# A table of C with one power of lambda more, and one product in place of two in a state-space scan

## The chip, the cores and the metric

The kernel runs on one core of a Trainium2 chip. Its time is the device time of one execution in microseconds (us). The engines of a core run their own instruction streams side by side and wait for each other by semaphores: TensorE (PE, matrix products), VectorE (DVE), ScalarE (ACT), GpSimd (POOL), and SyncE (SP), which here only issues transfers. POOL and ACT can issue transfers too. Each stream, and each queue of transfers issued from it, goes in order.

## The reference

Two layers of a streaming encoder. Each layer is half a feed-forward block, a mixer, and half a feed-forward block. In layer 0 the mixer is a diagonal state space (S5) beside attention. The change is in the S5 part:

```python
lam_bar = jnp.exp(lam * jnp.exp(log_step.astype(f32))[:, None])
b_bar = ((lam_bar - 1.0) / lam)[..., None] * lax.complex(b_re.astype(f32), b_im.astype(f32))
bu = jnp.einsum('gpc,btgc->btgp', b_bar, uf.astype(b_bar.dtype))
...
_, hs = lax.associative_scan(_lin_rec, (jnp.broadcast_to(lam_bar, bu.shape), bu), axis=1)
c = lax.complex(c_re.astype(f32), c_im.astype(f32))
y = jnp.einsum('gcp,btgp->btgc', c, hs).real + d.astype(f32).reshape(G_A, S5_GROUP) * uf
```

There are 32 groups of 16 channels with 64 complex states each.

## The kernel before, in words

The scan over time runs on blocks of four tokens. A state is carried from block to block, and what happens inside a block is put into tables that depend on the weights alone: E (powers of lambda times B-bar, 3 down to 0), C (C times the powers 1 to 4 of lambda), D (the response inside a block, C times powers 0 to 3 of lambda times B-bar, laid out as a block triangle), and cosines and sines for the rotation of the states. Sixteen pairs of groups have a table each. `s5_tables` (line 951) makes one and stores it in device memory (`S`); `s5_scan` (line 1017) later reads two at a time.

The tables are made beside the first feed-forward block (`ffn(0, 0, beside=...)` in `build`), whose inner loop runs 19 times through `head` (line 617, about 14.5 us each). After each head one step of the generator `tables()` is taken; `s5_tables` yields once, so that the second half of table e and the first half of table e+1 are recorded behind the same head. After four heads (three in the last groups) comes the output product `wout` (line 664), 35 us long. The order of the instructions within the engines' streams is set by a scheduler of the framework from its own estimates, not by the text alone; the listing below shows it.

The steps of a table, by line:

- 963, 964: two loads, on SP's queue, of B and C of this pair into `bc`.
- 969 (`cmul`, lines 875 to 880): six operations on POOL make B-bar (`bb`, 32 columns), with `tb` for scratch.
- 974: six operations on POOL make `E` (128 columns, scratch `tE`).
- 977: POOL makes `nci`, minus the imaginary part of C. 979: six operations on POOL write C into the table's tile `tab`.
- 986 to 992: ACT (L990) and DVE make the angles; 999: ACT writes cosine and sine into `tab`, 1000: POOL copies a part of them.
- 1005: two transposes of E on PE, 1006: ACT copies them into `tab`.
- 1010 to 1012: PE multiplies `bb` by C: power 0, straight from `bc` and `nci`, as 32 columns, and powers 1 to 3, from `tab`, as 96. Each has a real and an imaginary part: four matmuls in fp32, of two pieces each.
- 1014: four copies on ACT spread the result over the block triangle of D.
- 1015: POOL issues the store of `tab`.

`tab`, `bc`, `bb`, `nci` and the scratch tiles have one buffer each (`bufs=1`), so a table's step waits until the table before is done with the tile.

The lines of `head` that the text speaks of: ACT's copy at L637 hands a partial result on and frees PE's bank for the product of `S3` (L648, recorded as L550); DVE's L660 and L661 and ACT's L662 finish the head before. L460, L461 and L464 are the products of `unit_k` in `wout`, L321 and L322 the split of weights by ACT and DVE, and L373 the load of weights on SP's queue.

Of the kernel before, what the change touches and what calls it, by code (L numbers as in the profile page):

```python
# [26 lines left out]
NS = 173  # L27
# [11 lines left out]
def _layout(*items):  # L39
    d, o = {}, 0  # L40
    for n, k in items:
        d[n] = (o, k)
        o += k
    d["_n"] = o
    return d
# [8 lines left out]
C0 = _layout(("ident", 128), ("diag16", 16))  # L54
CA = _layout(("slot", 133), ("live", NS), ("msel", 1))
CB = _layout(("dbase", 528), ("dsamp", 528), ("dmeta", 16), ("cmb", 128))
CD = _layout(("tri", 128), ("tri16", 16), ("edge", 64), ("cos", 96), ("sin", 96), ("samp", 8))
SCAN = _layout(("ET", 256), ("C0", 128), ("C1", 128), ("D", 128), ("cos", NS), ("sin", NS))


def shape_constants():
# [209 lines left out]
class Kern:  # L271
# [679 lines left out]
    def s5_tables(self, pool, e):  # L951

        nc = self.nc
        v, g = nc.vector, nc.gpsimd
        P2 = slice(e, e + 1)

        def tl(name, sh, bufs=1, dt=F):
            return pool.tile([128] + sh, dt, name="st_" + name, tag=name, bufs=bufs)

        tab = tl("tab", [SCAN["_n"]])  # L960
        sub = lambda n: tab[:, SCAN[n][0]:SCAN[n][0] + SCAN[n][1]]
        bc = tl("bc", [4, 1, 32])
        nc.sync.dma_start(bc[:, 0:2], self.io["s5b"][:, :, P2])
        nc.sync.dma_start(bc[:, 2:4], self.io["s5c"][:, :, P2])

        bb = tl("bb", [2, 1, 32])
        tb = tl("tb", [1, 32])
        bx = lambda a: a[:, P2, None].to_broadcast([128, 1, 32])
        self.cmul(g, (bb[:, 0], bb[:, 1]), (bc[:, 0], bc[:, 1]), (bx(self.s5_co[0]), bx(self.s5_co[1])), tb)
        E = [tl(f"E{i}", [1, 4, 32]) for i in range(2)]  # L970
        tE = tl("tE", [1, 4, 32])
        ex = lambda a: a[:, P2, :, None].to_broadcast([128, 1, 4, 32])
        bxx = lambda a: a[:, :, None, :].to_broadcast([128, 1, 4, 32])
        self.cmul(g, E, (bxx(bb[:, 0]), bxx(bb[:, 1])), (ex(self.s5_rv[0]), ex(self.s5_rv[1])), tE)

        nci = tl("nci", [1, 32])
        g.tensor_scalar(nci, bc[:, 3], -1.0, None, op0=OP.mult)
        C = [sub(f"C{i}").rearrange("p (a j c) -> p a j c", a=1, j=4) for i in range(2)]
        self.cmul(g, C, (bxx(bc[:, 2]), bxx(nci)), (ex(self.s5_pw[0][:, :, 1:5]), ex(self.s5_npi[:, :, 1:5])), tE)
        D = sub("D").rearrange("p (a j c) -> p a j c", a=1, j=4)  # L980
        g.memset(D, 0.0)

        f0, f1, f2 = [tl(f"f{i}", [133]) for i in range(3)]
        th = slice(e, e + 1)

        def wrap(x):
            v.tensor_scalar(f1, x, MAGIC, MAGIC, op0=OP.add, op1=OP.subtract)
            v.tensor_tensor(x, x, f1, op=OP.subtract)

        nc.scalar.activation(f0, self.ca["slot"], AF.Copy, scale=self.s5_th[:, th])  # L990
        wrap(f0)
        v.scalar_tensor_tensor(f0, self.ca["slot"], self.s5_tl[:, th], f0, op0=OP.mult, op1=OP.add)
        v.tensor_scalar(f2, f0, 0.25, None, op0=OP.add)
        wrap(f0)
        wrap(f2)
        yield
        for n, x in (("cos", f2), ("sin", f0)):
            c = sub(n)
            nc.scalar.activation(c[:, 0:133], x, AF.Sin, scale=2.0 * PI_LIM)
            g.tensor_copy(c[:, 133:].rearrange("p (s k) -> p s k", k=5), c[:, None, 0:5].to_broadcast([128, 8, 5]))  # L1000

        pt = self.btile()[:, :256].rearrange("p (i a k) -> p i a k", i=2, a=1)
        for i in range(2):
            for a in range(1):
                nc.tensor.transpose(pt[:, i, a], E[i][:, a].rearrange("p i c -> p (i c)"), self.ident)
        nc.scalar.copy(sub("ET"), pt.rearrange("p i a k -> p (i a k)"))

        pk = self.btile()
        pkv = pk[:, :128].rearrange("p (a j c) -> p a j c", a=1, j=4)
        for j, c in ((0, (bc[:, 2, 0], nci[:, 0])), (1, [sub(f"C{i}")[:, 0:96] for i in range(2)])):  # L1010
            for i in range(2):
                nc.tensor.matmul(pk[:32, 32 * j:32 if j == 0 else 128], bb[:, i, 0], c[i], start=i == 0, stop=i == 1)
        for i in range(4):
            nc.scalar.copy(D[32 * i:32 * i + 32, :, i:4], pkv[:32, :, 0:4 - i])
        nc.gpsimd.dma_start(self.dram["S"][e], tab)

    def s5_scan(self, pool, e, U, G):

        nc = self.nc
        v, g = nc.vector, nc.gpsimd  # L1020
        P2 = slice(2 * e, 2 * e + 2)
        c4, pp0 = e // 2, 2 * (e % 2)

        def tl(name, sh, bufs=1, dt=F):
            return pool.tile([128] + sh, dt, name="sc_" + name, tag=name, bufs=bufs)

        tab = tl("tab", [2, SCAN["_n"]], 2)
        nc.sync.dma_start(tab, self.dram["S"][P2].rearrange("a p n -> p a n"))
        sub = lambda n: tab[:, :, SCAN[n][0]:SCAN[n][0] + SCAN[n][1]]
        ET = sub("ET").rearrange("p a (i k) -> p i a k", i=2)  # L1030
        C = [sub(f"C{i}") for i in range(2)]
        D = sub("D")
        cs = [sub(n) for n in ("cos", "sin")]
        u4 = tl("u4", [2, NS], 2)
        for i in range(4):
            nc.sync.dma_start(u4[32 * i:32 * i + 32],
                              U[c4, pp0 * 32:pp0 * 32 + 64, i].rearrange("(a c) s -> c a s", a=2))

        Z = [tl(f"Z{i}", [2, NS], 2) for i in range(2)]
        for i in range(2):  # L1040
            b = self.btile()
            for a in range(2):
                nc.tensor.matmul(b[:, a * NS:a * NS + NS], ET[:, i, a], u4[:, a], start=True, stop=True)
            nc.scalar.copy(Z[i].rearrange("p a s -> p (a s)"), b[:, :2 * NS])
        yield

        W = [tl(f"W{i}", [2, NS], 2) for i in range(2)]
        tmp = tl("tmp", [2, NS])
        sh = lambda t: t[:, :, 0:NS - 1]
        up = lambda t: t[:, :, 1:NS]  # L1050
        self.cmul(v, (up(W[0]), up(W[1])), (sh(Z[0]), sh(Z[1])), (up(cs[0]), up(cs[1])), sh(tmp), conj_b=True)
        for i, nm in enumerate(("h0re", "h0im")):
            g.memset(W[i][:, :, 0:1], 0.0)
            h0 = self.p[nm].rearrange("p (a b) -> p a b", b=8)
            g.tensor_copy(W[i][:, :, 133::5], h0[:, P2])
        mul = tl("mul", [2, NS])
        for a in range(2):
            v.tensor_scalar(mul[:, a], self.ca["live"], self.s5_r4[:, 2 * e + a:2 * e + a + 1], None, op0=OP.mult)
        fl = lambda t: t.rearrange("p a s -> p (a s)")
        for i in range(2):  # L1060
            v.tensor_tensor_scan(fl(W[i]), fl(mul), fl(W[i]), 0.0, op0=OP.mult, op1=OP.add)
        self.cmul(v, Z, W, cs, tmp)
        yield
        for i in range(2):
            g.tensor_copy(self.s5o[:, i, P2, 0:1], Z[i][:, :, 132:133])
            g.tensor_copy(self.s5o[:, i, P2, 1:9], Z[i][:, :, 137::5])
        b = self.btile()
        for a in range(2):
            q = b[:, a * NS:a * NS + NS]
            for i in range(2):  # L1070
                nc.tensor.matmul(q, C[i][:, a], Z[i][:, a], start=i == 0, stop=False)
            nc.tensor.matmul(q, D[:, a], u4[:, a], start=False, stop=True)
        y = tl("y", [2, NS], 2)
        for a in range(2):
            v.scalar_tensor_tensor(y[:, a], u4[:, a], self.p["d"][:, 2 * e + a:2 * e + a + 1], b[:, a * NS:a * NS + NS],
                                   op0=OP.mult, op1=OP.add)
        nc.scalar.activation(y, y, AF.Gelu_apprx_tanh)
        for j in range(4):
            nc.sync.dma_start(G[c4, pp0 * 32:pp0 * 32 + 64, j].rearrange("(a c) s -> c a s", a=2),
                              y[32 * j:32 * j + 32])  # L1080
        yield
# [923 lines left out]
def build(tc, io, stage=99, dbg=None):  # L2005
# [17 lines left out]
              "G": dr.tile([4, 128, 4, NS], F, name="G"), "LF": dr.tile([T, 8], F, name="LF"),  # L2023
              "M": dr.tile([128, 4, T], F, name="M"), "S": dr.tile([16, 128, SCAN["_n"]], F, name="S"), "FC": dr.tile([72, 528], F, name="FC"),
              "Q": dr.tile([8, 96, T], F, name="Q"), "K": dr.tile([8, 96, NP], F, name="K"),
# [354 lines left out]
```

## Time and profile before

| what | value |
|---|---|
| median of 3 runs | 2690.78 us (2679.24 to 2692.4) |
| the profiled execution | 2691.17 us |
| its span | 2689.0 us |
| PE busy | 2601.6 us, 97% of the span |
| DVE busy | 1958.2 us, 73% |
| ACT busy | 1169.4 us, 43% |
| POOL busy | 258.6 us, 10% |
| mean granted clock of PE | 0.989 of full speed |
| PE busy between 60 and 490 us | 417.67 of 430 us |

The span is what the profiler saw of the engines; the time of the execution is 2.17 us more. Almost all of the span is PE's own work, so its gaps are what other engines can cost. The chain of work that ended last is 81% PE, 7% DVE, 4% transfers, 2% POOL and 2% ACT. The tables' part on POOL lies in the first 470 us.

### The profile page before, as it was taken

Reading aid. Unit: us, or ns where it says so; the run is one execution under the profiler, and the core shown is the slowest. Engines: PE = TensorE matmul, PEld = TensorE weight load, DVE = VectorE, ACT = ScalarE, POOL = GpSimd, SP = SyncE. Lnnn points to the kernel's source line nnn. Section 1 sums busy time; section 2 is a strip of 40 time slices with the busy share of each in tenths; the row PEclk is TensorE's granted clock in tenths of the full one; section 3 lists DMA queues with packets and bytes.
Section 4 is the critical chain, followed back from the end, with each engine's and each line's share of the span. In section 5 each row is a group of like instructions: output and inputs, shape, how many; then the busy total and the mean of one; then the engine's idle time right before and its main releaser. Section 6 shows DMA issues by size and latency. Waiting matters only on the chain.

```text
span 2689.0 us, 45288 instructions
## 1 busy us (share of the span) xinstructions
PE 2601.6 (97%) x17467; PEld 2437.3 (91%) x17467; DVE 1958.2 (73%) x4011; ACT 1169.4 (43%) x2125; POOL 258.6 (10%) x572
## 2 busy tenths in 40 slices
PE   8999999998899999999999999999988999999999
PEld 8999999877679999999999999987766779999999
DVE  8778777887686867776887677766666667686776
ACT  6344444334553534333543334344544654343333
POOL 1046434031000000000000000002000100000000
PEclk9999999999999999999999999999998899999999
DMA  4233322545753222222222222244565532222222
GB/s 140 75 105 94 100 92 89 193 144 163 253 181 108 84 75 84 77 79 79 83 75 83 79 79 78 87 135 106 153 197 183 163 107 79 87 81 84 85 81 79
DMA packets 133172, 295.86 MB, mean 110 GB/s; under 512 B 30244, under 2 KB 55156, under 8 KB 128668
## 3 DMA queue, kind: packets, MB, share of 16 engines
q1 hardware_dynamic: 129516, 280.72, 33.6%
q0 software_dynamic: 2720, 10.78, 1.2%
q8 instruction: 138, 2.26, 0.3%
q10 hardware_dynamic: 720, 1.45, 0.2%
q14 instruction: 78, 0.64, 0.1%
HBM read 257.05 MB, written 34.21 MB: 108 GB/s over the span
## 4 chain that ended last, share of the span: by engine, by line
PE 81%; DVE 7%; DMA 4%; issue 4%; POOL 2%; ACT 2%; SPq 0%; DVEq 0%; ACTq 0%; POOLq 0%
PE pa L550 7%; PE pa L551 6%; PE pa L552 6%; PE pd L460 4%; PE pw L460 4%; PE pw L464 4%; PE pd L461 4%; PE pd L464 4%; PE pw L461 4%; PE pc L551 3%; PE pc L550 3%; PE pc L552 3%; PE pmm L464 2%; PE pmm L330 2%; PE pmm L461 2%
## 5 line engine op out<-in xcount | busy, mean ns | idle before, releaser
L321 ACT CAST whi<-wraw 128x1024 fp32r<-128x1024 f32 (+3 forms) x426 | 336.2, 790 | 654.8 <-PE pw L461 213.3
L322 DVE TENSOR_TENSOR wlo<-wraw,whi 128x1024 fp32r<-128x1024 f32 (+3 forms) x426 | 385.5, 906 | 132.8 <-ACT whi L321 126.4
L460 PE MATMUL pd<-gh,whi 128*128 128x328 f32 (+1 forms) x704 | 215.4, 313 | 0.5 <-ACT gh L321 0.3
L461 PE MATMUL pw<-gl,whi 128*128 128x328 f32 (+1 forms) x704 | 214.7, 312 | 0.0
L461 PE MATMUL pd<-gl,whi 128*128 128x328 f32 (+1 forms) x704 | 214.3, 312 | 0.0
L460 PE MATMUL pw<-gh,whi 128*128 128x328 f32 (+1 forms) x704 | 214.2, 311 | 0.0
L464 PE MATMUL pd<-gh,wlo 128*128 128x328 f32 (+1 forms) x704 | 162.8, 311 | 0.0
L464 PE MATMUL pw<-gh,wlo 128*128 128x328 f32 (+1 forms) x704 | 161.9, 311 | 0.0
L321 ACT CAST wvh<-wu 128x1024 fp32r<-128x1024 f32 x79 | 83.0, 1050 | 153.0 <-PE pc L551 150.7
L460 PEld LDWEIGHTS pd<-gh,whi 128*128 128x128 f32 x704 | 131.8, 188 | 3.4 <-ACT gh L321 1.4
L460 PEld LDWEIGHTS pw<-gh,whi 128*128 128x128 f32 x704 | 132.2, 188 | 0.2 <-issue 0.2
L461 PEld LDWEIGHTS pw<-gl,whi 128*128 128x128 f32 x704 | 132.3, 188 | 0.0
L461 PEld LDWEIGHTS pd<-gl,whi 128*128 128x128 f32 x704 | 132.0, 188 | 0.3 <-DVE gl L322 0.3
L672 DVE SCALAR_TENSOR_TENSOR mo<-pd,mo 128x328 f32<-128x328 f32 (+1 forms) x120 | 54.0, 492 | 106.3 <-PE pd L464 105.7
L330 PE MATMUL pmm<-whi,hh 128*128 128x512 f32 (+2 forms) x328 | 126.6, 389 | 2.3 <-ACT whi L321 2.3
L331 PE MATMUL pmm<-wlo,hh 128*128 128x512 f32 (+2 forms) x328 | 124.6, 380 | 0.8 <-DVE wlo L322 0.6
L332 PE MATMUL pmm<-whi,hl 128*128 128x512 f32 (+2 forms) x328 | 123.5, 376 | 0.0
L672 DVE SCALAR_TENSOR_TENSOR mo<-pw,mo 128x328 f32<-128x328 f32 (+1 forms) x120 | 54.0, 492 | 95.2 <-PE pw L464 95.1
L464 PEld LDWEIGHTS pd<-gh,wlo 128*128 128x128 f32 x704 | 118.9, 188 | 0.2 <-DVE wlo L322 0.2
L464 PEld LDWEIGHTS pw<-gh,wlo 128*128 128x128 f32 x704 | 118.8, 188 | 0.0
L550 PE MATMUL pa<-ht,wzh 128*128 128x328 f32 (+1 forms) x316 | 99.6, 315 | 6.1 <-ACT u L637 6.1
L550 PE MATMUL pa<-hh,whi 128*128 128x328 f32 (+1 forms) x316 | 100.6, 318 | 0.0
(659 smaller groups left out, 8042.5 us busy)
## 6 DMA issues: line engine op xcount, KB each, us to landing
wraw<-wi SPq DMA_DIRECT2D x97, 512.0 KB
wu<-wi SPq DMA_DIRECT2D x79, 512.0 KB
wraw<-wo SPq DMA_DIRECT2D x104, 256.0 KB
wraw<-wo SPq DMA_DIRECT2D x48, 320.0 KB
row<-dkT SPq DMA_DIRECT2D x8, 1024.0 KB
wraw<-ckT SPq DMA_DIRECT2D x16, 512.0 KB
row<-dv SPq DMA_DIRECT2D x8, 1024.0 KB
row<-fkT SPq DMA_DIRECT2D x8, 1024.0 KB
```

The lines of the kernel that those rows point to most:

```text
L321: nc.scalar.copy(hi, src)
L322: nc.vector.tensor_tensor(lo, src, hi.bitcast(F), op=OP.subtract)
L330: mm(ps, a[0], b[0], start=start, stop=False)
L331: mm(ps, a[0], b[1], start=False, stop=False)
L332: mm(ps, a[1], b[0], start=False, stop=stop)
L460: mm(ps[b], hi[:, ws], xh[:, c], start=start, stop=False)
L461: mm(ps[b], hi[:, ws], xl[:, c], start=False, stop=False)
L464: mm(ps[b], lo[:, ws], xh[:, c], start=False, stop=stop)
L550: nc.tensor.matmul(p[:, A], w[0][:, c], xh, start=start and i == 0, stop=False, skip_group_check=True)
L551: nc.tensor.matmul(p[:, A], w[0][:, c], xl, start=False, stop=False, skip_group_check=True)
L552: nc.tensor.matmul(p[:, A], w[1][:, c], xh, start=False, stop=i == 3, skip_group_check=True)
L672: v.scalar_tensor_tensor(self.x[:, o, c], p[b][:, A], 0.5, self.x[:, o, c], op0=OP.mult, op1=OP.add)
```

## The change

C gets power 0 of lambda too: five powers of 32 columns, 160 in place of 128, for the real and for the imaginary part. So the six operations at line 979 work on 160 columns, and `tE` is 160 wide. PE's product of `bb` and C then takes the first 128 of these columns (powers 0 to 3) in one piece for each part: two matmuls of 128 columns in place of two of 32 and two of 96, and none reads `bc` or `nci`. The table grows from 986 to 1050 numbers for each partition. `s5_scan` takes columns 32 to 160 of C (powers 1 to 4, as before).

```diff
-SCAN = _layout(("ET", 256), ("C0", 128), ("C1", 128), ("D", 128), ("cos", NS), ("sin", NS))
+SCAN = _layout(("ET", 256), ("C0", 160), ("C1", 160), ("D", 128), ("cos", NS), ("sin", NS))
...
-        C = [sub(f"C{i}").rearrange("p (a j c) -> p a j c", a=1, j=4) for i in range(2)]
-        self.cmul(g, C, (bxx(bc[:, 2]), bxx(nci)), (ex(self.s5_pw[0][:, :, 1:5]), ex(self.s5_npi[:, :, 1:5])), tE)
+        C = [sub(f"C{i}").rearrange("p (a j c) -> p a j c", a=1, j=5) for i in range(2)]
+        ex, bxx = [lambda a, f=f: f(a, 5) for f in (ex, bxx)]
+        self.cmul(g, C, (bxx(bc[:, 2]), bxx(nci)), (ex(self.s5_pw[0]), ex(self.s5_npi)), tE)
...
-        for j, c in ((0, (bc[:, 2, 0], nci[:, 0])), (1, [sub(f"C{i}")[:, 0:96] for i in range(2)])):
-            for i in range(2):
-                nc.tensor.matmul(pk[:32, 32 * j:32 if j == 0 else 128], bb[:, i, 0], c[i], start=i == 0, stop=i == 1)
+        for i in range(2):
+            nc.tensor.matmul(pk[:32, :128], bb[:, i, 0], sub(f"C{i}")[:, 0:128], start=i == 0, stop=i == 1)
...
-        C = [sub(f"C{i}") for i in range(2)]
+        C = [sub(f"C{i}")[:, :, 32:160] for i in range(2)]
```

(After the change the lines from 980 to the transposes stand one number higher; the product keeps its number, 1012.)

The order on POOL, from the end of C of table 1 to the first half of E of table 2, before:

```order
L880 TENSOR_TENSOR st_tab<-st_tab,st_tE 128x128
L1000 COPY st_tab<-st_tab 128x40 x2
L1015 DMA S<-st_tab 128x986
L875 TENSOR_TENSOR st_bb<-st_bc,s_cor 128x32
L876 TENSOR_TENSOR st_tb<-st_bc,s_coi 128x32
L878 TENSOR_TENSOR st_bb<-st_bc,s_cor 128x32
L877 TENSOR_TENSOR st_bb<-st_bb,st_tb 128x32
L977 TENSOR_SCALAR st_nci<-st_bc 128x32
L879 TENSOR_TENSOR st_tb<-st_bc,s_coi 128x32
L875 TENSOR_TENSOR st_E_1810<-st_bb,s_rv_945 128x128
L880 TENSOR_TENSOR st_bb<-st_bb,st_tb 128x32
L876 TENSOR_TENSOR st_tE<-st_bb,s_rv_946 128x128
```

and the same place after the change:

```order
L880 TENSOR_TENSOR st_tab<-st_tab,st_tE 128x160
L1001 COPY st_tab<-st_tab 128x40 x2
L876 TENSOR_TENSOR st_tb<-st_bc,s_coi 128x32
L977 TENSOR_SCALAR st_nci<-st_bc 128x32
L875 TENSOR_TENSOR st_bb<-st_bc,s_cor 128x32
L878 TENSOR_TENSOR st_bb<-st_bc,s_cor 128x32
L877 TENSOR_TENSOR st_bb<-st_bb,st_tb 128x32
L879 TENSOR_TENSOR st_tb<-st_bc,s_coi 128x32
L875 TENSOR_TENSOR st_E_1806<-st_bb,s_rv_945 128x128
L880 TENSOR_TENSOR st_bb<-st_bb,st_tb 128x32
L876 TENSOR_TENSOR st_tE<-st_bb,s_rv_946 128x128
L1015 DMA S<-st_tab 128x1050
```

The store of table 1 has moved behind nine operations of table 2.

The order on SP around the first loads of an output product, with the semaphores that each waits for (PE, Pool and DVE by their engine, DMAHW for a transfer), before:

```order
L373 DMA wraw<-wo 128x512 [waits DMAHW6_49,DVE_49]
L963 DMA st_bc<-s5b 128x2x32 [waits DMAHW4_49,DMAHW5_49,PE_49,Pool_49]
L964 DMA st_bc<-s5c 128x2x32 [waits DMAHW3_49]
L373 DMA wraw<-wo 128x512 [waits DMAHW7_49,DVE_49]
L373 DMA wraw<-wo 128x512 [waits DMAHW1_49,DVE_49]
```

and the same place after:

```order
L373 DMA wraw<-wo 128x512 [waits DMAHW6_49,DVE_49]
L963 DMA st_bc<-s5b 128x2x32 [waits DMAHW1_49,DMAHW0_49,Pool_49]
L373 DMA wraw<-wo 128x512 [waits DMAHW7_49,DMAHW5_49,DVE_49]
L964 DMA st_bc<-s5c 128x2x32
L373 DMA wraw<-wo 128x512 [waits DMAHW3_49,DVE_49]
```

The load of `bc` waits for POOL and no longer for PE, and its second half has moved behind a load of weights.

## Rows read from the trace of the kernel before

**Rows 1.** The page, section 1: busy us, share of the span, instructions.

```profile
PE 2601.6 (97%) x17467; PEld 2437.3 (91%) x17467; DVE 1958.2 (73%) x4011; ACT 1169.4 (43%) x2125; POOL 258.6 (10%) x572
```

**Rows 2.** Waits of PE, 130 to 470 us: total us, times, longest us.

```profile
PE pa L550 <- ACT u L637: 6.1, 7, 1.6
PE pb L1012 <- POOL st_tab L880: 3.5, 2, 2.2
```

**Rows 3.** The chain of waits, 205 to 262 us: start us, us, what.

```profile
208.84 0.22 PE pb L1005 x2
209.06 0.57 PE pb L1012 x8
...
211.12 5.58 DMA S<-st_tab
216.81 0.53 ACT st_tab L999 x2
217.36 0.42 ACT st_f L990
217.80 0.42 DVE st_f L987
...
221.13 0.75 ACT gs L662
221.88 0.33 ACT u L637
222.25 0.42 PE pa L550
```

**Rows 4.** Waits of ACT, 130 to 470 us.

```profile
ACT whi L321 <- PE pd L461: 34.4, 15, 3.0
...
ACT st_tab L999 <- DMA S<-st_tab: 9.3, 9, 2.0
```

**Rows 5.** Waits of DVE, 130 to 470 us.

```profile
DVE st_f L987 <- ACT st_f L990: 8.4, 10, 1.6
```

**Rows 6.** The store's line, L1015: what its engine waited for, and the landing.

```profile
  ACT st_tab L1014: 211.9, 15
...
DMA to landing us min/median/max: 3.1/3.6/5.6
```

**Rows 7.** Groups of instructions, POOL, 130 to 470 us: busy us, mean ns | idle before.

```profile
L876 POOL TENSOR_TENSOR st_tE<-st_bb,s_rv 128x128 f32<-128x128 f32 x15 | 8.6, 574 | 1.1
...
L875 POOL TENSOR_TENSOR st_E<-st_bb,s_rv 128x128 f32<-128x128 f32 x15 | 6.8, 456 | 0.0
...
L878 POOL TENSOR_TENSOR st_bb<-st_bc,s_cor 128x32 f32<-128x32 f32 x15 | 5.2, 350 | 0.0
...
L877 POOL TENSOR_TENSOR st_bb<-st_bb,st_tb 128x32 f32<-128x32 f32 x15 | 5.2, 345 | 0.0
L880 POOL TENSOR_TENSOR st_bb<-st_bb,st_tb 128x32 f32<-128x32 f32 x15 | 4.9, 328 | 0.0
L879 POOL TENSOR_TENSOR st_tb<-st_bc,s_coi 128x32 f32<-128x32 f32 x15 | 4.4, 292 | 0.1
L875 POOL TENSOR_TENSOR st_bb<-st_bc,s_cor 128x32 f32<-128x32 f32 x15 | 4.4, 292 | 5.9 <-DMA st_bc<-s5b 5.6
```

**Rows 8.** Timeline of POOL, a busy and a quiet stretch: start us, us, what.

```profile
227.25 0.29 POOL L875 TENSOR_TENSOR st_bb<-st_bc,s_cor 128x32 f32<-128x32 f32 x1
...
232.95 0.45 POOL L878 TENSOR_TENSOR st_E<-st_bb,s_rv 128x128 f32<-128x128 f32 x1
...
243.60 0.25 POOL L875 TENSOR_TENSOR st_bb<-st_bc,s_cor 128x32 f32<-128x32 f32 x1
...
245.91 0.40 POOL L878 TENSOR_TENSOR st_E<-st_bb,s_rv 128x128 f32<-128x128 f32 x1
```

**Rows 9.** Three windows: stretch, its us, busy us of each engine, PEclk, DMA share, GB/s.

```profile
222.00:226.00 4.00, 3.75 (x28) 3.42 (x29) 3.97 (x8) 3.58 (x9) 1.34 (x2) 1.00 0.42 131
241.00:245.00 4.00, 3.90 (x16) 3.73 (x17) 1.76 (x5) 0.86 (x5) 2.36 (x11) 0.57 0.58 177
245.00:249.00 4.00, 4.00 (x28) 4.00 (x27) 1.51 (x3) 2.21 (x6) 3.69 (x10) 1.00 0.08 32
```

**Rows 10.** Waits of SP's queue, 130 to 470 us.

```profile
SPq L963 <- PE pb L1012: 30.8, 11, 8.0
```

More of the change, by code (lines that the diff above doesn't have):

```diff
@@ L970, in s5_tables @@
         E = [tl(f"E{i}", [1, 4, 32]) for i in range(2)]
[L971 to L974, printed above, removed]
+        tE = tl("tE", [1, 5, 32])
+        ex = lambda a, n=4: a[:, P2, :, None].to_broadcast([128, 1, n, 32])
+        bxx = lambda a, n=4: a[:, :, None, :].to_broadcast([128, 1, n, 32])
+        self.cmul(g, E, (bxx(bb[:, 0]), bxx(bb[:, 1])), (ex(self.s5_rv[0]), ex(self.s5_rv[1])), tE[:, :, 0:4])
         nci = tl("nci", [1, 32])
         g.tensor_scalar(nci, bc[:, 3], -1.0, None, op0=OP.mult)
-        C = [sub(f"C{i}").rearrange("p (a j c) -> p a j c", a=1, j=4) for i in range(2)]
-        self.cmul(g, C, (bxx(bc[:, 2]), bxx(nci)), (ex(self.s5_pw[0][:, :, 1:5]), ex(self.s5_npi[:, :, 1:5])), tE)
+        C = [sub(f"C{i}").rearrange("p (a j c) -> p a j c", a=1, j=5) for i in range(2)]
+        ex, bxx = [lambda a, f=f: f(a, 5) for f in (ex, bxx)]
+        self.cmul(g, C, (bxx(bc[:, 2]), bxx(nci)), (ex(self.s5_pw[0]), ex(self.s5_npi)), tE)
         D = sub("D").rearrange("p (a j c) -> p a j c", a=1, j=4)
```

## The prediction

> **What bounds the kernel now.** I read the page's busy shares first: TensorE (PE) is busy for 2601.6 us of the 2689.0 us span, so a change pays only in PE's work or in the gaps of PE [rows 1]. All sixteen scan tables are built beside the first feed-forward block, between 130 and 470 us. PE's waits in that stretch are two lines and 9.6 us in all: 6.1 us, seven times, up to 1.6, for ScalarE's (ACT's) copy at L637, and 3.5 us, twice, up to 2.2, for GpSimd's (POOL's) last product of C at L880 [rows 2].
>
> The chain of waits shows where the longer line comes from [rows 3]. At 209.63 PE has finished the product at L1012 (209.06 + 0.57). At 211.12 POOL issues the store of that table, and it takes 5.58 us. The tile that it reads, `tab`, has one buffer; so ACT can't write the next table's cosine and sine (L999) before the store has landed, at 216.81. Behind L999, in order on ACT, stands L990, which VectorE (DVE) waits for (L987); behind that on DVE stand L660 and L661, then ACT's L662 and L637, and at 222.25 PE's product at L550, which had been idle for that 1.6 us. ACT waits for a store's landing nine times, 9.3 us in all, and DVE ten times for L990, 8.4 us [rows 4, 5]. So the landing of the store is on the path; the instant of its issue is a term of the sum.
>
> **The change, part by part.**
>
> *The product.* Before, it is four fp32 matmuls, eight pieces on PE, in 0.57 us; after, two of 128 columns, four pieces. A piece of 128 columns is bounded by the two transposes ahead of it, 0.22 us for two [rows 3]. Four are 0.44 us, so 0.13 us is saved for each table, 16 x 0.13 = 2.1 us. The bounds: nothing, if the pieces' start and not their columns sets the time, and 0.28 x 16 = 4.5 us, if each of the eight costs the same.
>
> *The six operations on C* grow from 128 to 160 columns. On POOL the same operation costs 0.292 us on 32 columns and 0.456 on 128 (L875's two groups), 0.0017 us a column: 0.055 us an operation and 0.33 us a table [rows 7]. They stand behind the landing of the store and ahead of PE's product some 14 us later; that slack hides them, except at the two tables where PE already waits for them, which are dealt with next.
>
> *The order on POOL* moves most, and the diff doesn't tell it. The product no longer reads `bc` and `nci` directly; so the next table's inputs can be loaded and POOL's next operations can start sooner. The listing shows what was made of it: ahead of the store of table e now stand nine operations of table e+1. Two of them (L876 on `tb`, L977) can run before PE's product; the other seven write `bb`, which PE's product still reads, so they can't start before it ends, and the store is behind them in POOL's queue. Before, the store waited only for ACT's four copies at L1014, which is most of POOL's idle time, 211.9 us in 15 waits [rows 6], and came 1.49 us after PE's product (209.63 to 211.12).
>
> The seven cost, by the mean of 15 each, 0.292 + 0.350 + 0.345 + 0.292 + 0.456 + 0.328 + 0.574 = 2.64 us [rows 7]. With some 0.25 us for PE's signal to reach POOL (estimated as half of the 0.5 us that lie between ACT's copies and the store) the store is issued 2.89 us after the product in place of 1.49: 1.40 us later. Two stretches bound this: all nine took 2.31 us in a quiet one (243.60 to 245.91) and 5.70 us in a busy one (227.25 to 232.95) [rows 8]; seven ninths of that are 1.8 and 4.4 us, so the store is 0.6 to 3.2 us later.
>
> The same nine operations on the same tiles thus take 2.5 times as long in the one stretch as in the other [rows 8]. [...] I take the mean of the fifteen and keep both ends.
>
> Where does the later landing cost? Of 15 stores that have a table after them, four land in the stage of the output product, where ACT's casts wait for PE up to 3.0 us at a time [rows 4]; there 1.4 us is hidden. Two follow a product that POOL made late, with ACT late as well; I count them at nothing. Nine remain, in which the chain of [rows 3] has no slack that I could find: 9 x 1.40 = **12.6 us**; 5.4 to 28 by the bounds.
>
> *What goes.* POOL starts the next table about 1.2 us earlier and has two operations behind it, while PE arrives later. The 3.5 us for L880 go. With the longer of the two goes a fall of PE's clock: from 241 to 245 it was granted 0.57 of full speed, between its two levels, and 16 matmuls began in 3.90 busy us, where at full clock 28 begin in 4.00 [rows 9]. Sixteen would take 2.3 us; 1.6 us are lost.
>
> *What comes.* The seven stalls at L550, 0.9 us in the mean and 1.6 at most, grow by 1.4, to 2.3 in the mean and 3.0 at most. Behind the stall of 1.6 us at 222 the granted clock was 1.00, behind the one of 2.2 it fell [rows 9]; of stalls that lie on both sides of the latter I count three with a fall, 3 x 1.6 = 4.8 us (none to seven: 0 to 11).
>
> *The inputs' load* on SyncE's (SP's) queue waited 30.8 us for PE's product [rows 10] and now waits for POOL's L879. In the stage of the output product a weight load stands behind it and comes some 3 us later; it is a load ahead, and ACT's cast of it waits for PE for up to 3.0 us anyway [rows 4]. I cost it at nothing, and at about 1 us in each of four stages, should the landing be late. The table is 6.5% larger (1050 numbers in place of 986): at most 0.065 x 3.6 = 0.2 us for a landing [rows 6], 9 x 0.2 = 2 us, in the range alone. In the scan itself the larger tables are loaded one ahead, beside the projections.
>
> **The sum**: 12.6 + 4.8 - 3.5 - 1.6 - 2.1 = +10.2 us. The profiled execution took 2691.17 us, 2.2 more than its span and 0.4 more than the median of the three runs, 2690.78; the sum stands against it: 2691.2 + 10.2 = 2701.4 us.
>
> **The rivals.**
>
> *A: the earlier start wins* (not slower). Place: the seven operations. If they run as in the quiet stretch (1.8 us), and in four of the nine heads DVE reaches L987 late by itself, the later store costs only 5 x 0.6 = 3 us, while 3.5 + 1.6 + 2.1 = 7.2 us go: 2687 us. It decides where the seven take less than about 2.1 us. For it: PE's longest wait on POOL and the fall of clock are certain losses of today. Against it: the mean of the fifteen is 2.64, and DVE waits for L990 ten times [rows 5].
>
> *B: a wash.* The seven cost the mean, but no clock falls, and two or three of the nine stores have slack: 7 x 1.4 - 7.2 = +2.6, 2694 us. For it: one of the nine stands where PE hardly waits; against it, the chain has DVE, ACT and PE back to back.
>
> *C: the store also lands later.* It is now issued in the thick of DVE's head. Landings range from 3.1 to 5.6 us, 3.6 in the median [rows 6]; if the nine went to 5.6, up to 2.0 us more each would come, and half of that, 9 us, with two more falls of clock (3.2 us), gives 2714 us. [...]
>
> **How the numbers follow.** Chances: my forecast 0.55 (2701, its own range 2694 to 2710), A 0.15, B 0.15, C 0.15. The time is 2701 us. The range takes in A's time and C's: 2686 to 2717. A measurement of this kernel tells about 0.5%, 13.5 us, from no change: below 2677 is faster, above 2704 slower. A is faster by that much in a third of its chance (0.05); the forecast passes 2704 in two fifths (0.22), and C does nearly always (0.14): slower 0.36. Left for within 0.5%: 0.59.
>
> **What would show it.** Right: the store (L1015) some 2 to 4 us after L1012 in place of 1.49; ACT's waits for its landing from 9.3 to 18 us or more; PE's waits at L550 from 6.1 to about 17 us, its waits at L1012 gone; spells of a granted clock under 1 behind the longest. Wrong: PE's waits at L550 as before, or the seven operations near 1.8 us everywhere (A), or a wait at L1012 that stays, or a difference in the span that lies after 490 us, on which I put none.

## The result, and the profile after

The changed kernel takes 2704.28 us (median of five runs, 2700.45 to 2711.06), where the kernel before, beside it on the same chip, took 2691.23 (median of five). The ratio is 1.0056, with a 95% interval of 1.004 to 1.0073: 11 to 20 us slower, 15 in the middle. The forecast was 2701. The profiled execution has a span of 2702.4 us, 13.4 more than that of before.

The page's busy shares after [rows 1]:

```profile
PE 2606.5 (96%) x17403; PEld 2439.9 (90%) x17403; DVE 1958.5 (72%) x4011; ACT 1168.5 (43%) x2125; POOL 263.5 (10%) x572
```

PE has 64 instructions fewer and 4.9 us more of busy time. The waits after, 130 to 485 us, of PE, ACT, DVE, POOL and SP's queue in turn (total us, times, longest us):

```profile
PE pa L550 <- ACT u L637: 19.0, 10, 2.5
...
ACT st_tab L1000 <- DMA S<-st_tab: 23.5, 13, 2.6
...
DVE st_f L988 <- ACT st_f L991: 18.9, 12, 3.1
...
POOL st_bb L875 <- PE pb L1012: 198.7, 15, 52.1
...
SPq L963 <- POOL st_tE L879: 57.3, 6, 9.6
```

PE's wait for the copy at L637 has grown from 6.1 to 19.0 us, and its 3.5 us for POOL are gone [rows 2]. ACT's wait for the store's landing went from 9.3 to 23.5 us [rows 4], and DVE's wait behind it from 8.4 to 18.9 [rows 5]. POOL's long wait is no longer that of the store for ACT's copies [rows 6]: it is that of the next table's first operation on `bb` for PE's product, and the store stands behind it.

One table after, on POOL from PE's product to the store (start us, us, what; in brackets the idle time before and its releaser). The product ran from 243.52 to 244.14:

```profile
244.23 0.93 POOL L875 TENSOR_TENSOR st_bb<-st_bc,s_cor 128x32 f32<-128x32 f32 x1 [1.92 <-PE pb L1012]
245.13 0.24 POOL L878 TENSOR_TENSOR st_bb<-st_bc,s_cor 128x32 f32<-128x32 f32 x1
...
246.55 0.70 POOL L880 TENSOR_TENSOR st_bb<-st_bb,st_tb 128x32 f32<-128x32 f32 x1
247.33 0.40 POOL L876 TENSOR_TENSOR st_tE<-st_bb,s_rv 128x128 f32<-128x128 f32 x1
247.67 0.62 POOL L1015 DMA_DIRECT2D S<-st_tab  x1
```

The same table goes on with ACT (the first, second, fourth and fifth row), DVE and PE:

```profile
251.41 0.52 ACT L1000 ACTIVATE st_tab<-st_f 128x133 f32<-128x133 f32 x2 [2.62 <-DMA S<-st_tab]
251.96 0.41 ACT L991 ACTIVATE st_f<-t_ca,s_th 128x133 f32<-128x133 f32 x1
...
252.41 0.56 DVE L988 TENSOR_SCALAR st_f<-st_f 128x133 f32<-128x133 f32 x1 [3.05 <-ACT st_f L991]
...
256.45 0.75 ACT L662 ACTIVATE gs<-gs 128x656 f32<-128x656 f32 x1 [3.14 <-DVE gs L661]
257.11 0.41 ACT L637 COPY u<-pa 128x328 f32<-128x328 f32 x1
...
257.58 0.64 PE L550 MATMUL pa<-ht,wzh 128*128 128x328 f32 x1 [2.44 <-ACT u L637]
```

It is the chain of [rows 3], link for link, with the store 3.53 us behind the product where it was 1.49, and 2.44 us of idle PE at its end. The windows behind four of the ten stalls, one of 1.80 us and the three longest (columns as in [rows 9]), show the clock that PE was granted between its two levels. They are 1.00 and 0.50: read in steps of 0.25 us, the third window has 1.00 to 257.25, 0.50 from 257.50 to 260.50, and 1.00 again from 260.75:

```profile
150.00:154.00 4.00, 3.34 (x15) 2.97 (x16) 3.97 (x8) 2.84 (x5) 1.24 (x2) 0.69 0.44 138
154.00:158.00 4.00, 4.00 (x25) 3.54 (x25) 2.36 (x6) 1.66 (x6) 2.73 (x8) 0.89 0.20 66
...
257.00:261.00 4.00, 3.42 (x13) 3.42 (x14) 3.21 (x5) 1.78 (x4) 0.75 (x1) 0.57 0.48 138
349.00:353.00 4.00, 3.97 (x16) 3.56 (x17) 3.22 (x7) 1.45 (x3) 0.16 (x1) 0.57 0.60 170
425.00:429.00 4.00, 3.98 (x18) 3.73 (x18) 3.08 (x7) 1.48 (x3) 0.00 (x0) 0.63 0.39 135
```

Where did the time go? From the start of the first table's product on PE to that of the fifteenth took 313.8 us before (137.29 to 451.13) and 326.8 after (137.23 to 464.03): 13.0 us, as much as the spans differ by. The loss lies beside the tables.

### The profile page after: what moved, and what is told of

Same layout as the page of the kernel before. It is cut to its first block, busy times and chain, and to the rows that moved or that the text cites. A ratio compares the mean times of both kernels' runs of the same rounds, so it can differ in the third digit from the quotient of the medians.

```text
span 2702.4 us, 45106 instructions
## 1 busy us (share of the span) xinstructions
PE 2606.5 (96%) x17403; PEld 2439.9 (90%) x17403; DVE 1958.5 (72%) x4011; ACT 1168.5 (43%) x2125; POOL 263.5 (10%) x572
## 5 line engine op out<-in xcount | busy, mean ns | idle before, releaser
L550 PE MATMUL pa<-ht,wzh 128*128 128x328 f32 (+1 forms) x316 | 101.9, 322 | 19.0 <-ACT u L637 19.0
L551 PE MATMUL pa<-ht,wzh 128*128 128x328 f32 (+1 forms) x316 | 100.4, 318 | 0.0
```

The source lines that it names most:

```text
L550: nc.tensor.matmul(p[:, A], w[0][:, c], xh, start=start and i == 0, stop=False, skip_group_check=True)
L551: nc.tensor.matmul(p[:, A], w[0][:, c], xl, start=False, stop=False, skip_group_check=True)
```

## The experiments

Theory 1: the store is late because it stands behind POOL's next table, and what is late in it comes out at PE. Rival 2: the wider C and the larger table cost it. Rival 3: the product of 128 columns is the slower. Theory 2a came with the second batch: POOL has so little slack ahead of PE's product that a longer C costs by itself. The times of before, 2686.76 to 2688.56 us, are those of the same chip and the same set of runs.

The table gives for each kernel how far the store's issue follows the end of PE's product (mean of ten tables: those that have another behind them in their group, without the fifteenth, behind which no run has a stall at L550), the stretch from the first to the fifteenth product less the 313.8 us of before, the waits of PE at L550 for L637, and the measured ratio. The first three are of one profiled execution each.

| kernel | store after product, us | stretch, us | waits at L550, us | ratio (interval) |
|---|---|---|---|---|
| before | 1.49 | 0 | 6.1 | 1 |
| after | 3.54 | +13.0 | 19.0 | 1.0056 (1.004 to 1.0073) |
| e1_old_product | 1.5 | +5.0 | 8.5 | 1.003 (1.0016 to 1.0044) |
| e2_store_first | 1.5 | +9.7 | 13.6 | 1.005 (1.0037 to 1.0064) |
| e3_four | 3.44 | +10.6 | 18.0 | 1.0038 (1.0025 to 1.005) |
| e4_bb2 | 3.98 | +17.5 | 21.9 | 1.0066 (1.0053 to 1.0079) |
| f1_late | 4.28 | +16.3 | 21.5 | 1.0072 (1.0055 to 1.0089) |
| f2_more | 1.5 | -0.4 | 7.5 | 0.9999 (0.9989 to 1.0009) |
| f3_size | 1.5 | +0.8 | 6.7 | 1.0006 (0.9997 to 1.0015) |
| f4_before_tab2 | 1.5 to 2.2 | +10.3 | 13.5 | 1.0039 (1.0026 to 1.0052) |
| g1_after_act | 1.0 (ACT) | -2.6 | 9.3 | 1.0003 (0.999 to 1.0016) |
| g2_before_act | 1.0 (ACT) | -5.3 | 4.0 | 0.9982 (0.9973 to 0.9991) |
| g3_wide_act | 1.0 (ACT) | -1.5 | 8.2 | 0.9999 (0.9989 to 1.001) |
| h1_more3 | 1.55 | +6.6 | 6.5 | 1.0027 (1.0015 to 1.0038) |

**e1_old_product.** The product of the kernel before, with the wide C.

```diff
-        for i in range(2):
-            nc.tensor.matmul(pk[:32, :128], bb[:, i, 0], sub(f"C{i}")[:, 0:128], start=i == 0, stop=i == 1)
+        for j, c in ((0, (bc[:, 2, 0], nci[:, 0])), (1, [sub(f"C{i}")[:, 32:128] for i in range(2)])):
+            for i in range(2):
+                nc.tensor.matmul(pk[:32, 32 * j:32 if j == 0 else 128], bb[:, i, 0], c[i], start=i == 0, stop=i == 1)
```

> C with five powers and the larger table, but the product takes its first 32 columns from bc and nci again, in four matmuls; POOL's order is that of the kernel before (the store ahead of the next table's operations). Theory 1 (the late store is the whole loss): within 2 us of the kernel before, 2689 to 2694; ACT's waits for the store's landing about 9 us, PE's waits at L550 about 6 us. Rival 2 (the wider C and the larger table cost it: six operations of 160 columns, 6.5% more to store and to load, and the 3 us that lie behind 500 us): 2697 to 2704.

2696.28 us, 4 to 12 over before: between what the two theories said. Theory 1 as the whole of the loss falls here. Of the 10.0 us by which the profiled execution is longer than that of before, 5.0 lie between the first and the fifteenth product. The other 5.0 lie behind it, in a stretch that runs from 2230.4 us (g2_before_act) to 2242.9 (this run) over the profiled executions of all these kernels.

**e2_store_first.** The whole change, with the next table's operations queued behind the store.

```diff
+        st = getattr(self, "s5_st", None)
+        with self.tc.issue_after(st) if st else ExitStack():
+            self.cmul(g, (bb[:, 0], bb[:, 1]), (bc[:, 0], bc[:, 1]), ...
...
+        self.s5_st = nc.gpsimd.dma_start(self.dram["S"][e], tab).ins
```

> The whole change, but the next table's first operations are queued behind the store, so that POOL's order is that of the kernel before. Theory 1: the loss goes, 2688 to 2693 (the kernel before less at most 3 us for a shorter product, plus nothing for C); store about 1.5 us after PE's product; waits at L550 about 6 us. Rival 2 (the wider C, the larger table): as after, 2700 to 2705. Rival 3 (a product of 128 columns is slower than the one of 32 and 96): 2700 to 2705 too, with e1_old_product at 2691.

2700.59 us: a miss for theory 1, which expected the loss to go. The edit gave the store its old place, but not SP's queue. Waits of e2, ACT and SP's queue, 130 to 490 us:

```profile
ACT whi L321 <- DMA wraw<-wo: 20.1, 4, 5.3
ACT st_tab L1003 <- DMA S<-st_tab: 13.4, 13, 2.8
...
SPq L963 <- POOL st_tE L879: 75.7, 6, 13.3
```

The load of `bc` now waits for POOL's L879 and not for PE's product [rows 10], for 75.7 us against 57.3 after the change, and the weight loads of the output product stand behind it: ACT's casts wait 20.1 us for them, 3.1 after the change. And the store, issued early, lands late: 3.9 us in the median and 5.8 at most, against 3.4 and 3.8 after the change. One table of e2 on SP's queue, POOL and ACT (start us, us, what):

```profile
151.43 0.54 SPq L587 DMA_DIRECT2D wu<-wi  x1
152.07 4.49 SPq L373 DMA_DIRECT2D wraw<-wo  x2
...
152.66 0.62 POOL L1018 DMA_DIRECT2D S<-st_tab  x1 [0.58 <-ACT st_tab L1017]
...
158.61 0.52 ACT L1003 ACTIVATE st_tab<-st_f 128x133 f32<-128x133 f32 x2 [2.80 <-DMA S<-st_tab]
```

The store goes out among three weight loads and ACT gets the table back 5.95 us later. So e2 is no clean test of the store's place.

**e3_four.** POOL's order of after, the product cut in two again:

```diff
+        for j, c in ((0, [sub(f"C{i}")[:, 0:32] for i in range(2)]), (1, [sub(f"C{i}")[:, 32:128] for i in range(2)])):
```

> The whole change and its order on POOL, but the product is cut into 32 and 96 columns of C again, four matmuls in place of two. Theory 1: as after, 2704 within 2 us, since the product's pieces took 0.57 us before and 0.62 after. The prediction's term (two matmuls save 0.13 us a table): 2706. Rival 3 (the product of 128 columns is the slower): 2700 or less.

2698.2 us, 7 to 13 over its before; the changed kernel is 11 to 20 over its own. The median is what rival 3 expected, and 6 us under that of theory 1, but the intervals overlap: by the times a product that costs some us cannot be excluded, and one that saves 2 us is not seen. PE's own rows speak against rival 3: from the product's start to the next matmul it is 0.57 us in e3 and 0.55 in the changed kernel, in the median of sixteen tables.

**e4_bb2.** Two buffers for `bb` in the changed kernel, so that nothing on POOL waits for PE's product.

```diff
-        bb = tl("bb", [2, 1, 32])
+        bb = tl("bb", [2, 1, 32], 2)
```

> The whole change, with two buffers for bb: POOL's operations of the next table no longer wait for PE's product, and run ahead of it; the store again waits for ACT's four copies only. Theory 1: the store about 1.5 us after PE's product, waits at L550 at most 6 us, 2686 to 2692. Theory 1 with POOL's early work in the way of DVE: up to 2697. Rivals 2 and 3: 2700 to 2705.

2704.75 us, the opposite of what was expected. The scheduler put still more of the next table ahead of the store. POOL in e4 (start us, us, what; the product ended at 229.25):

```profile
232.38 0.79 POOL L880 TENSOR_TENSOR st_E<-st_E,st_tE 128x128 f32<-128x128 f32 x1
233.25 0.79 POOL L876 TENSOR_TENSOR st_tE<-st_nci,s_npi 128x160 f32<-128x160 f32 x1
233.99 0.62 POOL L1015 DMA_DIRECT2D S<-st_tab  x1
```

The store comes 4.7 us after the product. So the edit missed its aim, and became a second dose of the same cause: a later store, a longer stretch.

**f1_late.** The kernel before, with nothing changed but the instant of the store:

```diff
+        for _ in range(6):
+            g.tensor_copy(D, D)
         nc.gpsimd.dma_start(self.dram["S"][e], tab)
```

> The kernel before, with six copies of D onto itself on POOL between ACT's four copies and the store, so that the store alone comes some 2 us later; product, C and the table's size are those of before. Theory 1 (a later store costs what ACT waits for its landing): 8 to 13 us more than the kernel before, nearly all of it between 130 and 490 us, waits at L550 15 to 20 us. Rival 2 (the loss is that of the wider C and the larger table alone): within 3 us of the kernel before.

2707.04 us against 2688.56: 15 to 24 us more, where 8 to 13 were expected for a store some 2 us later. PE's waits in f1, 130 to 490 us:

```profile
PE pa L550 <- ACT u L637: 21.5, 10, 2.6
PE pb L1012 <- POOL st_tab L880: 0.8, 1, 0.8
```

With product, C and table as before, a store 2.8 us later (4.28 in place of 1.49) gives the stalls of after, ten times at L550. A late store, without the wider C and without the new product, makes such a loss; this is shown. The six copies also keep POOL busy for 2.4 us a table and put the next table's operations off, but PE hardly waits for those (0.8 us).

**f2_more**, one copy of C's real part for each table on POOL ahead of the product, 0.38 us in the median and 0.56 in the mean:

```diff
+        g.tensor_copy(C[0], C[0])
```

> The kernel before, with one more POOL operation for each table, a copy of C's real part onto itself ahead of its last product: about 0.3 us, as much as the six wider operations add; the table keeps its size and the store its place. Theory 2a (POOL is late with C at some tables, so that longer operations put PE's product off): 3 to 6 us more than before, waits at L1013 of 4 us or more, or more tables with C ready within 1 us of the product. Rival 2b (the larger table costs it): within 2 us of before.

2687.91 us: no difference, within 3 us. **f3_size**, the larger table alone:

```diff
-        g.memset(D, 0.0)
+        g.memset(tab[:, SCAN["pad"][0]:SCAN["pad"][0] + 192], 0.0)
```

> The kernel before, with 64 columns of zeros beside D in the table: 1050 numbers are stored and loaded, as after the change, the operations on C are those of before, and the memset of D is 192 columns in place of 128. Theory 2a: within 2 us of before. Rival 2b (6.5% more to store, and to load ahead of the scan): 4 to 8 us more, with landings of the store longer than 3.6 in the median, or losses behind 490 us.

2689.56 us, 1 less to 4 more than before: 6.5% more to store and to load costs nothing that shows.

**f4_before_tab2.** Two buffers for the table in the kernel before:

```diff
-        tab = tl("tab", [SCAN["_n"]])
+        tab = tl("tab", [SCAN["_n"]], 2)
...
+        f2, f0 = [sub(n)[:, 0:133] for n in ("cos", "sin")]
...
+        tE = sub("ET")[:, 0:128].rearrange("p (a j c) -> p a j c", a=1, j=4)
```

> The kernel before, with two buffers for tab, so that ACT's cosine and sine of the next table wait for no landing of a store (room is made by building f0, f2 and tE inside the table, which gives them two buffers too). Theory 1: waits of ACT for a landing gone, waits at L550 from 6 us to 2 or less, the chain of DVE and ACT from the landing gone: 4 to 9 us less than before. Rival (POOL or DVE is the next that is late): within 3 us of before, with the waits of PE on other engines as large.

2698.37 us, 7 to 14 slower where 4 to 9 faster was expected. Waits of ACT in f4, 130 to 490 us:

```profile
ACT st_tab L1000 <- DVE st_tab L989: 34.3, 23, 4.3
...
ACT st_tab L991 <- DMA S<-st_tab: 11.2, 12, 1.8
```

ACT's wait for a landing moved to L991, and a longer one for DVE's work on the angles came ahead of it: they now lie in the table. The edit changed two things at once and says little on theory 1.

**g1_after_act and g2_before_act.** The store is issued by ACT, behind its own copies, in the changed kernel and in the one before:

```diff
-        nc.gpsimd.dma_start(self.dram["S"][e], tab)
+        nc.scalar.dma_start(self.dram["S"][e], tab)
```

> The whole change, but the store is issued by ACT, right behind its four copies of PE's product, and not by POOL: nothing of POOL's next table stands ahead of it any more, with POOL's order else as after the change. Theory 1: the loss of 13 us goes, for the store leaves some 1 us after the product: 5 us less to 3 us more than the kernel before; waits at L550 8 us or less. Theory 2a (C's longer operations and the product): 4 to 9 us more than before stay, with waits of PE for C. Rival (the store's place is only a symptom): 11 to 15 us more than before.

> The kernel before with the same edit. Theory 1: the store leaves 0.5 us earlier, 5 us less than before if each of nine tables gains 0.5, and more if a store from ACT's queue also lands sooner than one from POOL's (3.6 us in the median); waits at L550 3 us or less. Rival: ACT, which now issues it, is held by the issue, and nothing is gained: within 3 us of before.

g1 takes 2687.71 us against 2686.76, 3 less to 4 more: the loss against the kernel before is gone, with C, table, product and the first operations of POOL's next table as after the change. Waits of ACT and PE in g1, 130 to 490 us:

```profile
ACT st_tab L1000 <- DMA S<-st_tab: 5.7, 6, 2.5
...
PE pa L550 <- ACT u L637: 9.3, 10, 1.9
```

That a store from ACT's queue lands sooner is not seen: in the six tables where ACT waited for it, ACT had the table back 3.0 to 6.6 us after the issue, and 3.3 to 3.9 us in the thirteen of the changed kernel. What the rows show gained is the instant of the issue, 1.0 us after the product in place of 3.54.

g2 takes 2682.81 us, 2 to 7 less than before: it beats both kernels. It also shows that g1 has gained more than the change had lost by the store's place, since ACT's issue comes 0.5 us sooner than that of before. Beside g2, which has that too, g1 is still 4.9 us slower (between 1 and 10 by the two intervals), with 9.3 us of waits at L550 against 4.0: some 5 us of the change do not hang on POOL's queue. PE's waits in g2, 130 to 490 us (those of before are in [rows 2]):

```profile
PE pa L550 <- ACT u L637: 4.0, 8, 0.8
PE pb L1012 <- POOL st_tab L880: 1.3, 1, 1.3
```

and two of its rows on ACT, the last copies of a product and the issue:

```profile
250.72 0.89 ACT L1014 COPY st_tab<-pb 32x128 f32<-32x128 f32 x4 [0.20 <-PE pb L1012]
251.69 0.33 ACTq L1015 DMA_DIRECT2D S<-st_tab  x1
```

The issue takes 0.33 us of ACT's queue, at 1.0 us after the product.

**h1_more3**, three copies where f2 had one, and **g3_wide_act**, which is e1 with the store on ACT:

> The kernel before with three copies of C's real part onto itself for each table on POOL, some 1.2 us ahead of PE's product, where f2_more had one. Theory 2a (POOL has little slack ahead of the product, and what C takes longer comes out at PE at the later tables of a group): 6 to 12 us more than before, waits at L1014 of 6 us or more. Rival (a slack of some 3 us for all but two tables): 0 to 4 us more.

> As e1_old_product (wider C and larger table, product in four matmuls from bc and nci, POOL's order of before), with the store issued by ACT as in g2_before_act. Theory 2a (the six wider operations cost by themselves, since POOL is late with C): 3 to 8 us more than g2_before_act stood against the kernel before, so 2 us less to 3 us more than before, waits of PE for POOL's C 3 us or more. Rival (the 8 us of e1_old_product were not those of the wider operations, and what g1_after_act has over g2_before_act is the new product's): 3 to 6 us less than before, as g2_before_act.

h1 takes 2694.12 us, 4 to 10 more. Its waits of PE, 130 to 490 us:

```profile
PE pb L1014 <- POOL st_tab L981: 7.4, 3, 2.7
PE pa L550 <- ACT u L637: 6.5, 8, 1.3
```

The copies took 0.52 us each in the mean. So some 1.6 us more of POOL's work ahead of the product comes out at PE, as a wait for C itself, though 0.6 us (f2) did not. g3 takes 2687.52 us, 3 less to 3 more than before, where g2 was 2 to 7 less: the wide C takes back about 4.6 us (0.9999 less 0.9982), between 1 and 8. Theory 2a expected that. But PE hardly waits for C in g3. Its waits, 60 to 500 us:

```profile
PE pa L550 <- ACT u L637: 8.2, 10, 1.8
...
PE pb L1013 <- POOL st_tab L880: 0.3, 2, 0.2
```

The 4.6 us come out at L550 (8.2 us against 4.0 in g2), so the way from the wider operations to PE isn't the one that theory 2a named. The traces show where the time is: in DVE's operations on the angles, which stand ahead of L660 and L661. All of them (112 of each kernel, 130 to 490 us) took 40.6 us in g2 and 44.3 in g3, and 40.8 us before and 45.8 in e1. One group of them, in g2 and then in g3:

```profile
L987 DVE TENSOR_SCALAR st_f<-st_f 128x133 f32<-128x133 f32 x42 | 11.8, 281 | 5.6 <-ACT st_f L990 5.3
...
L988 DVE TENSOR_SCALAR st_f<-st_f 128x133 f32<-128x133 f32 x42 | 14.1, 336 | 7.3 <-ACT st_f L991 7.0
```

In both e1 and g3, then, the wider operations on POOL go with slower operations on DVE beside them; that the one makes the other was not tried by itself.

## Why the prediction was right, and where only the sum was

*The store's place: the right mechanism, three sizes off that cancelled.* The term was 9 stores times 1.40 us, 12.6; PE's waits at L550 grew by 12.9 (19.0 less 6.1). That the two agree so closely is luck: more tables paid, the delay was longer, and each us of it cost less than a us. The instant: 3.54 us after the product and not 2.89, so 2.05 us later. The seven operations took 3.08 us by their means and not 2.64; POOL began 0.09 us after the product (244.14 to 244.23), where 0.25 were estimated, and the rest lies between the operations. Four of the groups after, 130 to 485 us (columns as in [rows 7]):

```profile
L875 POOL TENSOR_TENSOR st_E<-st_bb,s_rv 128x128 f32<-128x128 f32 x15 | 9.3, 619 | 0.0
...
L880 POOL TENSOR_TENSOR st_bb<-st_bb,st_tb 128x32 f32<-128x32 f32 x15 | 7.8, 518 | 0.0
...
L875 POOL TENSOR_TENSOR st_bb<-st_bc,s_cor 128x32 f32<-128x32 f32 x15 | 7.3, 485 | 198.7 <-PE pb L1012 198.7
...
L878 POOL TENSOR_TENSOR st_bb<-st_bc,s_cor 128x32 f32<-128x32 f32 x15 | 4.3, 284 | 0.0
```

They were 456, 328, 292 and 350 ns [rows 7]: of these four one is faster, three are 1.4 to 1.7 times as long in their new place in the head of a table. The longer end of the prediction, from its busy stretch, was 3.2 us later; the 2.05 of the trace lie between it and the mean's 1.40. The slow row at 244.23 (0.93 us) ran beside this one of DVE, which has two inputs and ended 0.09 us sooner (start us, us, what):

```profile
244.23 0.84 DVE L322 TENSOR_TENSOR gl<-us,gh 128x656 fp32r<-128x656 f32 x1
```

Other rows go the same way: of POOL's 89 two-input operations on 128 x 32 elements after the change (130 to 485 us), the 49 that began while DVE ran a TENSOR_TENSOR that reads none of PE's banks took 0.57 us in the mean, the other 40 took 0.24. The two go together in this trace; that the one makes the other slow was not tried by itself.

The slope: ten stores 2.05 us later would be 20.5 us if nothing had slack, and ACT's wait for the landing grew by 14.2 (23.5 less 9.3). The step "no slack that I could find" was wrong: the kernel before often had some. By f1, 2.79 us on each of ten stores made 16.3 us of stretch, 0.6 us for each us; at that price the 20.5 us are worth 12, nearly all of the 13.0.

*The two late products, counted at nothing.* They are the third tables of their groups, at 243.52 and 334.99, and with 410.92 they have the longest stalls of all, 2.4 to 2.5 us. After the change POOL is early with C there (4.4 us ahead of the product), so nothing else was late, and the store's delay came out in full. Ten tables pay, not nine: eight of the nine, and these two; the ninth, the fifteenth table of all, has no stall at L550 behind it.

*What goes.* The 3.5 us at L1012 went, as forecast: POOL's early start did that.

*The clock.* Counted: three new falls, one gone, 3.2 us. Seen: four, in the windows above. By the working of the prediction (28 matmuls in 4.00 us at full clock [rows 9]) they lost 1.6 us (15 and 25 matmuls in 7.34), 1.6, 1.7 and 1.4, 6.3 in all; with the fall of before gone, +4.7. They are behind the longest stalls, as forecast, and behind one of 1.80 us; behind one of 1.84 the granted clock stayed at 1.00, so the length of the stall alone did not decide.

*The product: mis-sized.* -2.1 us were counted at 0.11 us a piece. After, the next matmul begins 0.55 us after the product's start (243.52, 244.07); in g2, which has the old product, 0.57 us after it:

```profile
250.04 0.25 PE L1012 MATMUL pb<-st_bc,st_bb 128*32 128x32 f32 x2
250.12 0.23 PE L1012 MATMUL pb<-st_nci,st_bb 128*32 128x32 f32 x2
250.19 0.50 PE L1012 MATMUL pb<-st_tab,st_bb 128*32 128x96 f32 x4
250.61 0.42 PE L460 MATMUL pd<-gh,whi 128*128 128x328 f32 x1
```

That is 0.02 us a table, 0.3 us in all: both products have 512 columns over all their pieces (2 x 32, 2 x 32 and 4 x 96, or 4 x 128), and half the pieces are each twice as long (0.55 / 4 against 0.57 / 8).

These terms make 12.9 - 3.5 + 4.7 - 0.3 = 13.8 us, where the stretch of the tables grew by 13.0.

*The six wider operations: counted at nothing.* In POOL's old order they have a price: about 4.6 us by g3 and g2, 4 to 12 by e1, though neither the larger table (f3) nor 0.6 us more on POOL (f2) shows it. There the prediction's reason, slack ahead of PE's product, was not enough, for the time is lost at L550 and not at the product. In the changed kernel no such term is seen: PE never waits for C, the six take 3.20 us a table where they took 3.64 before, by the sums of their means, and DVE's operations on the angles take 37.6 us where they took 40.8. The sum above comes out without it. But g1 against g2 says that some 5 us stay with the store on ACT, so a price of nothing is not shown for it either.

*The larger table and the inputs' load*, both at nothing: the first held (f3). The second held in the changed kernel (3.1 us of ACT's time, once); in e2 it did not.

*Rival C* (the store also lands later) is refuted. The landing after, from the store's line [rows 6]:

```profile
DMA to landing us min/median/max: 3.1/3.4/3.8
```

It was 3.1/3.6/5.6: the longest is shorter by 1.8 us, though the store is now issued 2 us further into DVE's head. *Rival A* needed seven operations of less than 2.1 us, and they took 3.08. *Rival B* needed a clock that doesn't fall, and it fell four times; it was right that some stores have slack.

What is shown: the loss against before goes when the store leaves POOL's queue (g1), and such a loss comes when the store is late with nothing else of the change (f1). What stays open: how much of e1's 4 to 12 us is the wider C. Its profile has 5.0 us beside the tables, and the slower DVE there is read from the traces, not tried. Open too is what makes g1 5 us slower than g2, and whether the product of 128 columns costs some us elsewhere than on PE (e3 against the changed kernel is within the intervals).

## What to carry to other kernels

A dependence that an edit takes away is also an order that it takes away: look in the listing at what a scheduler pulls ahead of the instruction that was last in a queue, and price the wait of those pulled ahead, not only their work. Where the landing of a transfer frees a buffer, try to issue it from the queue of the engine that writes that buffer last, so that nothing stands between; here one word moved it from POOL to ACT, undid the loss, and made the kernel before faster too. Taking more dependences away did not help in either trial: a second buffer for `bb` let still more work ahead of the store (e4), and a second buffer for the table, with the angles moved into it, cost 7 to 14 us (f4).

## What was not expected

- Issued later, the store landed sooner: 3.4 us in the median and 3.8 at most after the change, where it was 3.6 and 5.6. The three longest of before (5.58, 5.21 and 4.88 us, issued at 211.12, 300.89 and 315.83) were issued 0.5 us behind a weight load (210.61, 300.38 and 315.32), one at 226.62, as close behind one, took 3.96, and the store of e2 above, with ACT's 5.95 us, stands among three; that these are the cause was not tried.
- The same POOL operation on 128 x 32 elements took 0.24 us and 0.93 in one table (the rows at 244.23 and 245.13): the duration of this operation, read in one place, did not hold for the other.
- A store from ACT's queue took 0.33 us of that queue, from POOL's 0.62.
